# Hybrid attention layer: compressed keys and values as a fifth seven-product pair, other homes for its sums, one compression input on GpSimd

## Chip, core and metric

The kernel runs on one core of a Trainium2 chip. The metric is the device time of one execution in microseconds, median of the runs. Everything is float32 at full precision.

## What is computed

One decoder layer on 1024 tokens of width 1024: native sparse attention (NSA) and latent attention (MLA) side by side, merged by sigmoid gates, then a gated FFN with a short convolution. The change concerns the projections of the first half:

```python
h = _rmsnorm(x, g_pre_mix[i])
proj = h @ w_in[i]
q_n, kv_n, gate_n, c_q, c_kv, k_r, merge = jnp.split(proj, offsets, axis=-1)
...
def compress(k, pos, w1, b1, w2):
    kb = k[:, blk] + pos[None, None, :, None, :]
    kb = kb.transpose(0, 1, 3, 2, 4).reshape(B, n_cmp, G, CMP_BLOCK * dh)
    return jax.nn.gelu(kb @ w1 + b1) @ w2
k_cmp = compress(kc, pos_k, ck_w1, ck_b1, ck_w2)
v_cmp = compress(vc, pos_v, cv_w1, cv_b1, cv_w2)
...
gm = jax.nn.sigmoid(merge.astype(jnp.float32)).astype(x.dtype).reshape(B, T, 2, D)
merged = gm[:, :, 0] * (o_nsa @ w_br_nsa[i]) + gm[:, :, 1] * (o_mla @ w_br_mla[i])
```

kc and vc are columns 512 to 639 and 640 to 767 of `w_in`; the merge gates are 16 blocks of 128 columns from column 1720.

## The kernel before, in words

**Precision.** TensorE multiplies float32 tiles rounded to a shorter format. To keep full precision each operand is split into a rounded high part and a low rest, and each product is three matmuls: high by high, low by high, high by low (`mm3`, lines 303 to 305). The split is a pair: ScalarE writes the high part, VectorE subtracts (`split_evac`, lines 308 and 309; for whole weights lines 106 and 107, tiles whi and wlo). h, transposed, stays in SBUF as hh and hl in two halves of 512 tokens.

**Weights.** One queue in the order of use, loaded by SP into three raw buffers (wraw, 512 KB each). A whole projection of a 128-column block, `fproj`, is 8 x 3 matmuls for each half of the tokens, 48 in all. For gates that fill in between other work it is cut into eight quarters of six matmuls each, which `some(n)` hands out.

**Seven products.** Two 128-column blocks together go through class `Seven`: a pair is treated as a 2 x 2 block product that needs seven block products instead of eight, each 4 x 3 matmuls, 84 per pair. The data side needs sums T1 to T4 of h's blocks (lines 736 to 753, split into T1h, T1l and so on); the weight side needs sums S0 to S3 (line 170), which like the plain weight halves are split into a ring of four rh and rl; the outputs are put together by VectorE (line 194) in two tiles `gms`. Four pairs of gates (`gates7.pair`) are done so, then sent through a sigmoid and stored to DRAM (gm_d).

**Order around the change.** First the MLA branch: q blocks (six matmuls each) with quarters of gates between them, then k and v blocks (three matmuls each) with quarters, each split into one of six store buffers (st) and stored by SP (qn_d, qr_d, k_d, v_d). Then the last quarters, the four gate pairs, the projections of kc and vc into kcT0 and kcT1, and for keys and values in turn: `cmp_build` (loads, a transpose of pos, and kb = kcT + pos, four operations of 64 x 1008, line 858), the projection of other k columns (`k_evac`, into KA and KB), and `cmp_mm`, 16 float32 matmuls that the page counts as 32 instructions (line 865). Then the eight values blocks (V), `cmp_out` (lines 868 to 879: the second step of the compression and its splits into KAc, KBc, Vc), the q projections and the attention. GpSimd prepares constant rows of KB, KBc and of QB (lines 891 to 901 and 949 to 955).

A scheduler orders each engine's instructions; each engine then runs its own in that order and waits where an input or a buffer is not ready. Tiles get addresses from stacks on the left and the right side, so a tile can lie where an earlier one lay, and its first writer waits for the last user of that memory, stores to DRAM included.

Of the kernel before, what the change touches and what calls it, by code (L numbers as in the profile page):

```python
# [17 lines left out]
T = 1024  # L18
# [257 lines left out]
def tile_hybrid_layer(ctx: ExitStack, tc: tile.TileContext, x, p, positions, g_pre_mix, w_in,  # L276
# [85 lines left out]
    for c0 in [512, 640, 768, 1024]:  # L362
        W.add(Item(in_cols(c0), 1024))
# [404 lines left out]
    for i in range(4):  # L768
        c, g = i // 2, i % 2
        for f, n in ((q_nope(2 * g, c), 1), (q_rope(g, c), 2), (q_nope(2 * g + 1, c), 1)):  # L770
            f()
            some(n)
# [15 lines left out]

    ringA = Pool("ringA", side="left")
    tB = Pool("tB", side="left")  # L790
    for n in ("T3", "T4"):
        BA[n] = [tB([128, 4, 512], F32R, n + tag) for tag in "hl"]
    gates7 = Seven(nc, W, gate_pairs, ringA, BA, mm3, split_evac)
    t_first(2)()
    some(4)
    t_first(3)()
    some(4)
# [6 lines left out]
    for f in range(len(gate_pairs)):  # L804
        tl = [gmp([128, T], F32, "gms", bufs=2) for _ in range(2)]
        gates7.pair(f, two_banks(), bank, lambda shape, dt, name: eA(shape, dt, "t2", bufs=4), [(c[:, :512], c[:, 512:]) for c in tl],
                    lambda out_, ps: nc.scalar.activation(out_, ps, AF.Sigmoid), lambda s: None)
        nc.scalar.activation(tl[1], tl[1], AF.Sigmoid)
        nc.scalar.dma_start(gm_d[PAIRED[2 * f + 1]], tl[1])
        nc.scalar.activation(tl[0][:, 512:], tl[0][:, 512:], AF.Sigmoid)  # L810
        nc.scalar.dma_start(gm_d[PAIRED[2 * f]], tl[0])
    for pl in (tB, ringA, tA, eA):
        pl.close()
# [15 lines left out]
    kcT = [cp([128, T], F32, f"kcT{n}") for n in range(2)]  # L829
    for n in range(2):  # L830
        fproj(lambda c, cs, ps, n=n: nc.scalar.activation(kcT[n][:, cs], ps, AF.Copy))

    kbs, w1s, b1s = [], [], []

    def cmp_build(n):
        pos, w1, b1, w2 = ((nsa_pos_k, nsa_ck_w1, nsa_ck_b1, nsa_ck_w2),
                           (nsa_pos_v, nsa_cv_w1, nsa_cv_b1, nsa_cv_w2))[n]
        pl = cp([32, 2, 64], F32, f"pos{n}")
        nc.scalar.dma_start(pl[:, 0], pos[0])
        nc.scalar.dma_start(pl[:, 1], pos[0])  # L840
        w1t = cp([128, 16, 64], F32, "w1t")
        nc.scalar.dma_start(w1t, dap(w1, 0, [[64, 128], [128 * 64, 16], [1, 64]]))
        nc.scalar.dma_start(w2s[n][:, 0], w2[0])
        nc.scalar.dma_start(w2s[n][:, 1], w2[0])
        b1t = cp([64, 1], F32, f"b1t{n}")
        nc.scalar.dma_start(b1t, dap(b1, 0, [[1, 64], [1, 1]]))
        ps = bank()
        nc.tensor.transpose(ps[:, :32], pl.rearrange("p a b -> p (a b)"), ident[:32, :32])
        posT = cp([128, 32], F32, f"posT{n}")
        nc.vector.tensor_copy(posT, ps[:, :32])  # L850
        kb = cp([128, 16, 126], F32, "kb")
        for g in range(2):
            for par in range(2):
                src = kcT[n][g * 64:(g + 1) * 64, :]
                src = bass.AP(tensor=src.tensor, offset=src.offset + par,
                              ap=[list(src.ap[0]), [2, 16], [16, 63]])
                pp = posT[g * 64:(g + 1) * 64, par:32:2]
                nc.vector.tensor_tensor(kb[par * 64:(par + 1) * 64, :, g * 63:(g + 1) * 63], src,
                                        pp[:, :, None].to_broadcast([64, 16, 63]), op=OP.add)
        kbs.append(kb), w1s.append(w1t), b1s.append(b1t)  # L860
# [56 lines left out]
    for t in range(NT):  # L917
        ps = bank()
        for k in range(NK):
            mm3(ps[:, :256], tok(hh, k, t), tok(hl, k, t), w2[k // 4][0][:, k % 4], w2[k // 4][1][:, k % 4],  # L920
                k == 0, k == NK - 1)
        v = VV[t // 4][:, t % 4]
        split_evac(v[:, :, 0:64], v[:, :, 64:128], ps[:, :256].rearrange("p (a b) -> p a b", b=64))
    cmp_out()
# [998 lines left out]
```

## Time and profile before

| | |
|---|---|
| median of 3 runs | 1753.53 us (1749.5 to 1753.94) |
| profiled execution, its own time | 1752.63 us |
| its span | 1750.8 us |
| busy: TensorE, VectorE, ScalarE, GpSimd | 1694.3, 1262.1, 851.7, 304.1 us |
| mean granted clock of TensorE | 0.99 |

In the profile PE is TensorE's matmuls and PEld its weight loads, DVE is VectorE, ACT ScalarE, POOL GpSimd, SP the engine that issues most DMAs. A row of the timeline gives start and duration in us, engine, line, operation, output<-inputs, shape, count and, in brackets, how long the engine was idle before and what released it. TensorE's rows overlap: a 128x512 matmul lasts 0.39 us and the next starts after 0.23. In a table of stretches the engines come in the order PE, PEld, DVE, ACT, POOL.

### The profile page before, as it was taken

The numbers are of one execution on the slowest core, as the hardware profiler recorded it, in microseconds if no ns is written. First come the engines' busy times: TensorE is split into PE (matmuls) and PEld (weight loads), VectorE is DVE, ScalarE is ACT, GpSimd is POOL, SyncE is SP. The second block draws the span as 40 slices with busy tenths as digits, with TensorE's granted clock in tenths as the row PEclk, the third lists the DMA queues.
The fourth block names the chain that finished last, engine by engine and source line by source line (L and its number), as shares of the span: only waits on it lengthen the run. The fifth ranks groups of instructions, "written<-read, shape, count | busy, mean of one in ns | idle before, by whom it ended". The sixth has DMA issues, their size and how long they took to land.

```text
span 1750.8 us, 23413 instructions
## 1 busy us (share of the span) xinstructions
PE 1694.3 (97%) x8468; PEld 1394.1 (80%) x8468; DVE 1262.1 (72%) x1981; ACT 851.7 (49%) x1537; POOL 304.1 (17%) x446
## 2 busy tenths in 40 slices
PE   8999999999999999998999999999999999999998
PEld 6887888887777888886778877888888877887786
DVE  5667735238989888777755797888888779868543
ACT  5434423237777677666432454444444454335321
POOL 4100022014555453333211000000000000001110
PEclk9999999999999999999999999999999999999999
DMA  5266332100003237656462122222222393437111
GB/s 198 66 238 229 104 108 57 37 30 13 1 1 91 73 95 184 156 155 182 136 217 84 57 64 73 84 85 76 84 94 73 112 316 125 143 122 255 58 61 48
DMA packets 166670, 191.93 MB, mean 110 GB/s; under 512 B 13348, under 2 KB 116188, under 8 KB 166556
## 3 DMA queue, kind: packets, MB, share of 16 engines
q1 hardware_dynamic: 158732, 178.29, 33.0%
q10 hardware_dynamic: 7824, 12.16, 2.0%
q8 instruction: 67, 1.10, 0.3%
q14 instruction: 47, 0.39, 0.1%
HBM read 142.96 MB, written 47.45 MB: 109 GB/s over the span
## 4 chain that ended last, share of the span: by engine, by line
PE 78%; DVE 9%; DMA 5%; ACT 3%; issue 2%; POOL 1%; SPq 0%; DVEq 0%; POOLq 0%; ACTq 0%
PE big L303 9%; PE big L304 9%; PE big L305 9%; PE pT L303 6%; PE pT L305 6%; PE pT L304 5%; PE oT L1015 5%; PE pT L999 4%; PE one L303 3%; PE one L304 3%; PE one L305 3%; PE sc L305 2%; PE sc L303 2%; PE sc L304 2%; DVE wlo L309 2%
## 5 line engine op out<-in xcount | busy, mean ns | idle before, releaser
L345 POOL TENSOR_SCALAR stat<-stat 128x1 f32<-128x1 f32 (+1 forms) x48 | 15.0, 313 | 887.9 <-ACT yn L1404 633.6
L303 PE MATMUL big<-hh,rh 128*128 128x512 f32 x380 | 148.2, 390 | 2.5 <-ACT e L220 1.0
L304 PE MATMUL big<-hl,rh 128*128 128x512 f32 x380 | 148.0, 389 | 0.0
L305 PE MATMUL big<-hh,rl 128*128 128x512 f32 x380 | 147.5, 389 | 0.0
L309 DVE TENSOR_TENSOR pl<-pT,ph 128x512 fp32r<-128x512 f32 x228 | 139.1, 626 | 11.4 <-ACT ph L308 9.5
L308 ACT ACTIVATE ph<-pT 128x512 fp32r<-128x512 f32 x228 | 120.6, 553 | 47.7 <-PE pT L999 36.0
L983 DVE TENSOR_REDUCE mx<-sc 128x1 f32<-128x640 f32 (+7 forms) x128 | 106.6, 835 | 28.9 <-PE sc L1068 19.8
L308 ACT ACTIVATE rh<-S 128x512 fp32r<-128x512 f32 x96 | 60.3, 629 | 110.1 <-PE big L304 78.0
L1527 DVE SCALAR_TENSOR_TENSOR u<-C,wcT,u 128x1024 f32<-128x1024 f32 x88 | 110.9, 1280 | 3.7 <-ACT u L1523 3.2
L308 ACT ACTIVATE rh<-wraw 128x512 fp32r<-128x512 f32 x80 | 50.0, 630 | 107.7 <-PE big L304 47.1
L304 PE MATMUL big<-wlo,whi 128*128 128x512 f32 x242 | 95.5, 395 | 5.8 <-DVE wlo L309 5.8
L305 PE MATMUL big<-whi,wlo 128*128 128x512 f32 x242 | 94.9, 392 | 0.0
L303 PE MATMUL big<-whi 128*128 128x512 f32 x242 | 91.5, 394 | 1.7 <-ACT whi L308 1.7
L303 PEld LDWEIGHTS big<-hh,rh 128*128 128x128 f32 x380 | 71.2, 188 | 18.6 <-ACT e L220 1.5
L304 PEld LDWEIGHTS big<-hl,rh 128*128 128x128 f32 x380 | 71.3, 188 | 15.1 <-DVE hl L309 0.4
L305 PEld LDWEIGHTS big<-hh,rl 128*128 128x128 f32 x380 | 71.3, 188 | 14.7
L309 DVE TENSOR_TENSOR rl<-S,rh 128x512 fp32r<-128x512 f32 x96 | 65.7, 688 | 20.2 <-ACT rh L308 20.1
L303 PE MATMUL pT<-hh,whi 128*128 128x512 f32 x176 | 69.7, 396 | 2.3 <-DVE KBc L874 2.0
L308 ACT ACTIVATE whi<-wraw 128x1024 fp32r<-128x1024 f32 x40 | 42.1, 1058 | 59.8 <-DVE wraw L1593 25.9
L305 PE MATMUL pT<-hh,wlo 128*128 128x512 f32 x176 | 69.4, 394 | 0.0
L304 PE MATMUL pT<-hl,whi 128*128 128x512 f32 x176 | 69.2, 393 | 0.0
L309 DVE TENSOR_TENSOR rl<-wraw,rh 128x512 fp32r<-128x512 f32 x80 | 54.7, 687 | 11.4 <-ACT rh L308 11.4
(565 smaller groups left out, 5044.3 us busy)
## 6 DMA issues: line engine op xcount, KB each, us to landing
wraw<-in_w_up_dram SPq DMA_DIRECT2D x44, 512.0 KB, 4.0
wraw<-in_w_in_dram SPq DMA_DIRECT2D x24, 512.0 KB, 4.5
g<-gm_d SPq DMA_DIRECT2D x48, 256.0 KB, 3.5
wraw<-in_w_down_dram SPq DMA_DIRECT2D x47, 256.0 KB, 3.5
g_d<-u SPq DMA_DIRECT2D x22, 512.0 KB, 2.6
wraw<-g_d SPq DMA_DIRECT2D x36, 256.0 KB, 3.0
gm_d<-gms ACTq DMA_DIRECT2D x16, 512.0 KB, 2.9
xt<-in_x_dram SPq DMA_DIRECT2D x14, 512.0 KB, 3.7
```

Of the source, the lines that this page charges most:

```text
L303: nc.tensor.matmul(ps, lh, rh, start=start, stop=False, skip_group_check=more)
L304: nc.tensor.matmul(ps, lh, rl, start=False, stop=False, skip_group_check=more)
L305: nc.tensor.matmul(ps, ll, rh, start=False, stop=stop, skip_group_check=more)
L308: nc.scalar.activation(hi, ps, AF.Copy)
L309: nc.vector.tensor_sub(lo, ps, f32(hi))
L345: nc.gpsimd.tensor_scalar(st, st, EPS, None, op0=OP.add)
L983: nc.vector.tensor_reduce(u.nm[:, r:r + 1], src, axis=AX.XY, op=OP.max, negate=True)
L999: nc.tensor.transpose(pT[:m, r], cols(r), ident)
L1015: nc.tensor.matmul(oT[:, a:], v, part_, start=first and not j, stop=last and j == len(parts) - 1)
L1527: nc.vector.scalar_tensor_tensor(u[s], C[s][:, 2 - sh:2 - sh + T], wcT[:, 2 - sh, ch:ch + 1], u[s], op0=OP.mult, op1=OP.add)
```

## The change

Columns 512 and 640 leave the list of whole projections and become a fifth pair of `Seven`; its evacuation copies where the others take the sigmoid, and its two output tiles are kcT. The quarters between the q blocks become one each (12 instead of 16), those at the end six and six (12 instead of 8). T3 and T4 are taken from the stack before the ring, T4 first. The twelve loads of `cmp_build` go from ScalarE's queue to SP's, with buffers of their own for w1t and kb. The values' kb is computed on GpSimd. `cmp_out` is called at the fourth of the values blocks instead of after the eighth.

```diff
     gate_pairs = [[W.add(Item(in_cols(1720 + 128 * m), 1024, custom=True)) for m in (m_, m_ + 1)] for m_ in PAIRED[::2]]
-    for c0 in [512, 640, 768, 1024]:
+    gate_pairs.append([W.add(Item(in_cols(c0), 1024, custom=True)) for c0 in (512, 640)])
+    for c0 in [768, 1024]:
         W.add(Item(in_cols(c0), 1024))
...
-        for f, n in ((q_nope(2 * g, c), 1), (q_rope(g, c), 2), (q_nope(2 * g + 1, c), 1)):
+        for f in (q_nope(2 * g, c), q_rope(g, c), q_nope(2 * g + 1, c)):
             f()
-            some(n)
+            some(1)
...
+    tB = Pool("tB", side="left")
+    for n in ("T4", "T3"):
+        BA[n] = [tB([128, 4, 512], F32R, n + tag) for tag in "hl"]
     ringA = Pool("ringA", side="left")
-    tB = Pool("tB", side="left")
-    for n in ("T3", "T4"):
-        BA[n] = [tB([128, 4, 512], F32R, n + tag) for tag in "hl"]
     gates7 = Seven(nc, W, gate_pairs, ringA, BA, mm3, split_evac)
     t_first(2)()
-    some(4)
+    some(6)
     t_first(3)()
-    some(4)
+    some(6)
...
+        way = AF.Copy if f == 4 else AF.Sigmoid
         gates7.pair(f, two_banks(), bank, lambda shape, dt, name: eA(shape, dt, "t2", bufs=4), [(c[:, :512], c[:, 512:]) for c in tl],
-                    lambda out_, ps: nc.scalar.activation(out_, ps, AF.Sigmoid), lambda s: None)
+                    lambda out_, ps: nc.scalar.activation(out_, ps, way), lambda s: None)
+        if f == 4:
+            kcT = tl
+            break
...
-    kcT = [cp([128, T], F32, f"kcT{n}") for n in range(2)]
-    for n in range(2):
-        fproj(lambda c, cs, ps, n=n: nc.scalar.activation(kcT[n][:, cs], ps, AF.Copy))
...
-        w1t = cp([128, 16, 64], F32, "w1t")
-        nc.scalar.dma_start(w1t, dap(w1, 0, [[64, 128], [128 * 64, 16], [1, 64]]))
-        nc.scalar.dma_start(w2s[n][:, 0], w2[0])
-        nc.scalar.dma_start(w2s[n][:, 1], w2[0])
+        w1t = cp([128, 16, 64], F32, f"w1t{n}")
+        nc.sync.dma_start(w1t, dap(w1, 0, [[64, 128], [128 * 64, 16], [1, 64]]))
+        nc.sync.dma_start(w2s[n][:, 0], w2[0])
+        nc.sync.dma_start(w2s[n][:, 1], w2[0])
...
-        kb = cp([128, 16, 126], F32, "kb")
+        kb = cp([128, 16, 126], F32, f"kb{n}")
...
-                nc.vector.tensor_tensor(kb[par * 64:(par + 1) * 64, :, g * 63:(g + 1) * 63], src,
+                (nc.gpsimd if n else nc.vector).tensor_tensor(kb[par * 64:(par + 1) * 64, :, g * 63:(g + 1) * 63], src,
                                         pp[:, :, None].to_broadcast([64, 16, 63]), op=OP.add)
...
+        if t == 3:
+            cmp_out()
         v = VV[t // 4][:, t % 4]
         split_evac(v[:, :, 0:64], v[:, :, 64:128], ps[:, :256].rearrange("p (a b) -> p a b", b=64))
-    cmp_out()
```

The lines after the change stand one or two further down than before. At three places the order of an engine's rows carries the argument.

ScalarE from the split of the last v block (the st row of shape 128x8x64) to the ring's first splits, before. DMAHW and a number is the completion of a transfer on one of the DMA rings, the other names are engines; gms is a finished half of a gate.

```order
L308 ACTIVATE st<-pT 128x8x64 [waits DMAHW5_49,DVE_49,PE_49]
L629 ACTIVATE gms<-sc 128x512 [waits PE_49]
L631 DMA gm_d<-gms 128x1024 [waits Activation_49]
L308 ACTIVATE T3h<-e 128x512 [waits DMAHW3_49,DMAHW4_49,DMAHW2_49,DVE_49]
L308 ACTIVATE T4h<-t_1471 128x512
L308 ACTIVATE rh<-wraw 128x512 [waits DMAHW0_49]
L308 ACTIVATE rh<-wraw 128x512 [waits DMAHW7_49]
L308 ACTIVATE rh<-S_1623 128x512 [waits DVE_49]
```

And in the changed kernel:

```order
L308 ACTIVATE st<-pT 128x8x64 [waits DMAHW3_49,PE_49]
L630 ACTIVATE gms<-sc 128x512 [waits PE_49]
L632 DMA gm_d<-gms 128x1024 [waits DMAHW4_49,Activation_49]
L630 ACTIVATE gms<-sc 128x512 [waits DMAHW5_49,PE_49]
L308 ACTIVATE T3h<-e 128x512 [waits DMAHW7_49,DMAHW0_49,DVE_49]
L308 ACTIVATE T4h<-t_1445 128x512
L308 ACTIVATE rh<-wraw 128x512 x2
L308 ACTIVATE rh<-S_1623 128x512 [waits DVE_49]
L308 ACTIVATE rh<-S_1617 128x512
L630 ACTIVATE gms<-sc 128x512 [waits PE_49]
```

Before, two halves of a gate and its store stand ahead of T3h; now the second half comes after the ring's splits, and T3h waits on other transfers.

VectorE at the values' kb (kb_2493, before); KB10 and KB11 are split from the second k columns, and wlo belongs to the values' weights.

```order
L858 TENSOR_TENSOR kb_2493<-kcT1_2227,posT1_2491 64x16x63 x3
L887 TENSOR_TENSOR KB01_2209<-pT_2431,KA01_2205 64x512
L858 TENSOR_TENSOR kb_2493<-kcT1_2227,posT1_2491 64x16x63
L887 TENSOR_TENSOR KB10_2210<-pT_2504,KA10_2206 64x512
L887 TENSOR_TENSOR KB11_2211<-pT_2504,KA11_2207 64x512
L107 TENSOR_TENSOR wlo_2598<-wraw_2297,whi_2597 128x1024
L887 TENSOR_TENSOR KB10_2210<-pT_2535,KA10_2206 64x512
L887 TENSOR_TENSOR KB11_2211<-pT_2535,KA11_2207 64x512
```

GpSimd in the changed kernel at the same place, from the constant rows of KBc to the first row of the attention's preparation.

```order
L902 TENSOR_SCALAR KBc0_2354<-jrow_2366 1x64
L902 TENSOR_SCALAR KBc1_2355<-jrow_2366 1x64
L897 MEMSET KB00_2348 1x1024
L898 TENSOR_SCALAR KB00_2348<-jrow_2366 1x1024
L897 MEMSET KB01_2349 1x1024
L898 TENSOR_SCALAR KB01_2349<-jrow_2366 1x1024
L897 MEMSET KB10_2350 1x1024
L898 TENSOR_SCALAR KB10_2350<-jrow_2366 1x1024
L897 MEMSET KB11_2351 1x1024
L898 TENSOR_SCALAR KB11_2351<-jrow_2366 1x1024
L859 TENSOR_TENSOR kb1_2514<-gms_2216,posT1_2512 64x16x63 x4
L969 TENSOR_SCALAR QB10_3125<-QA1_2616 64x512
```

kb1 has left VectorE's rows and stands on GpSimd behind all the constant rows of KB.

VectorE around `cmp_out` (KBc and Vc), before; V1 is the second half of the values, wlo the weights of the first q columns.

```order
L309 TENSOR_TENSOR V1_2596<-pT_2738,V1_2596 128x4x64
L309 TENSOR_TENSOR V1_2596<-pT_2765,V1_2596 128x4x64
L107 TENSOR_TENSOR wlo_2839<-wraw_2398,whi_2838 128x1024
L309 TENSOR_TENSOR V1_2596<-pT_2792,V1_2596 128x4x64
L107 TENSOR_TENSOR wlo_2845<-wraw_2502,whi_2844 128x1024
L874 TENSOR_TENSOR KBc0_2214<-pT_2819,KAc0_2212 64x63
L309 TENSOR_TENSOR Vc0_2198<-pT_2825,Vc0_2198 63x64
L309 TENSOR_TENSOR Vc1_2199<-pT_2831,Vc1_2199 63x64
L874 TENSOR_TENSOR KBc1_2215<-pT_2819,KAc1_2213 64x63
```

And in the changed kernel:

```order
L309 TENSOR_TENSOR V0_2340<-pT_2705,V0_2340 128x4x64
L875 TENSOR_TENSOR KBc0_2354<-pT_2730,KAc0_2352 64x63
L309 TENSOR_TENSOR Vc0_2338<-pT_2736,Vc0_2338 63x64
L875 TENSOR_TENSOR KBc1_2355<-pT_2730,KAc1_2353 64x63
L309 TENSOR_TENSOR Vc0_2338<-pT_2736,Vc0_2338 63x64
L309 TENSOR_TENSOR Vc1_2339<-pT_2742,Vc1_2339 63x64 x2
L309 TENSOR_TENSOR V1_2617<-pT_2750,V1_2617 128x4x64
L309 TENSOR_TENSOR V1_2617<-pT_2777,V1_2617 128x4x64
L309 TENSOR_TENSOR V1_2617<-pT_2804,V1_2617 128x4x64
L107 TENSOR_TENSOR wlo_2860<-wraw_2419,whi_2859 128x1024
L309 TENSOR_TENSOR V1_2617<-pT_2831,V1_2617 128x4x64
```

The two wlo that stood ahead of the first KBc row now stand after the Vc rows, with three V rows between.

## Rows read from the trace of the kernel before

**Rows 1.** The page's busy times, and the chain that ended last by engine.

```profile
PE 1694.3 (97%) x8468; PEld 1394.1 (80%) x8468; DVE 1262.1 (72%) x1981; ACT 851.7 (49%) x1537; POOL 304.1 (17%) x446
...
PE 78%; DVE 9%; DMA 5%; ACT 3%; issue 2%; POOL 1%; SPq 0%; DVEq 0%; POOLq 0%; ACTq 0%
```

**Rows 2.** Stretches: length, busy us of each engine (instructions), granted clock, DMA share, GB/s.

```profile
162.00:172.00 10.00, 6.09 (x14) 4.31 (x15) 7.42 (x13) 5.13 (x10) 0.00 (x0) 0.66 0.51 158
172.00:232.00 60.00, 60.00 (x266) 49.65 (x265) 41.94 (x65) 26.12 (x42) 0.00 (x0) 1.00 0.35 106
```

**Rows 3.** The chain that ended last, 157 to 167 us: start, us, what.

```profile
157.43 6.38 DMA v_d<-st
...
163.91 0.64 ACT T3h L308
...
164.58 0.59 DVE T3l L309
...
166.47 0.61 DVE rl L309
```

**Rows 4.** TensorE's timeline, 155 to 172 us: start, us, what, [idle before <-releaser].

```profile
155.59 0.39 PE L305 MATMUL pT<-wvh,ctl 128*128 128x512 f32 x1
...
161.61 0.39 PE L305 MATMUL sc<-hh,wlo 128*128 128x512 f32 x1
165.64 0.80 PE L303 MATMUL sc<-hh,rh 128*128 128x512 f32 x1 [3.64 <-ACT rh L308]
...
171.99 0.40 PE L304 MATMUL pT<-hl,rh 128*128 128x512 f32 x1
```

**Rows 5.** The timelines of TensorE and of VectorE around `cmp_out`.

```profile
320.25 0.28 PE L305 MATMUL pT<-whi,hl 128*128 128x256 f32 x1
...
321.88 0.33 PE L877 MATMUL pT<-w2t,gl 64*63 64x64 f32 x2 [0.69 <-DVE V L309]
324.19 0.47 PE L303 MATMUL pT<-hh,whi 128*128 128x512 f32 x1 [1.98 <-DVE KBc L874]
...
329.07 0.40 PE L305 MATMUL pT<-hh,wlo 128*128 128x512 f32 x1
...
320.27 1.23 DVE L107 TENSOR_TENSOR wlo<-wraw,whi 128x1024 fp32r<-128x1024 f32 x1 [1.74 <-ACT whi L106]
...
321.92 1.23 DVE L107 TENSOR_TENSOR wlo<-wraw,whi 128x1024 fp32r<-128x1024 f32 x1
```

**Rows 6.** Stretches of the q section and of the last stores, columns as above.

```profile
115.00:120.00 5.00, 5.00 (x24) 4.14 (x23) 4.83 (x8) 0.91 (x2) 0.00 (x0) 1.00 0.24 91
156.00:162.00 6.00, 5.75 (x24) 4.43 (x24) 2.92 (x5) 0.68 (x2) 0.00 (x0) 1.00 1.02 365
```

**Rows 7.** The chain that ended last at the first compression.

```profile
278.48 3.60 PE pT L865 x32
```

**Rows 8.** Groups of GpSimd and VectorE, shapes apart, and line 955 (ns min/median/max).

```profile
L965 POOL TENSOR_TENSOR QB<-QB,inc 1x512 fp32r<-1x512 f32 x12 | 12.4, 1032 | 12.1 <-PE sc L1035 8.6 <-PE sc L1037 3.1
L1332 POOL TENSOR_TENSOR g<-g,g 128x512 f32<-128x512 f32 x8 | 11.1, 1393 | 23.7 <-DVE g L1330 8.3 <-DVE pl L309 7.9 <-DMA g<-gm_d 7.6
...
L313 POOL TENSOR_TENSOR oml<-osum,omh 64x512 fp32r<-64x512 f32 x8 | 10.7, 1333 | 12.2 <-ACT omh L312 12.2
...
L313 POOL TENSOR_TENSOR wol<-wlo,woh 128x1024 fp32r<-128x1024 f32 x1 | 3.4, 3397 | 0.0
...
L309 DVE TENSOR_TENSOR rl<-S,rh 128x512 fp32r<-128x512 f32 x96 | 65.7, 688 | 20.2 <-ACT rh L308 20.1
...
L858 DVE TENSOR_TENSOR kb<-kcT,posT 64x1008 f32<-64x1008 f32 x8 | 15.1, 1890 | 0.2
...
L955 POOL TENSOR_SCALAR QB<-PC x16: 288/290/1867, 254.6 to 273.5; 1x128 fp32r<-1x128 f32 x16
```

**Rows 9.** GpSimd's timeline, the last of four fills of KB.

```profile
263.90 0.95 POOL L896 MEMSET KB<- 1x1024 f32 x1
264.91 1.04 POOL L897 TENSOR_SCALAR KB<-jrow 1x1024 fp32r<-1x1024 f32 x1
```

More of the change, by code (lines that the diff above doesn't have):

```diff
@@ L811, in tile_hybrid_layer @@
         nc.scalar.dma_start(gm_d[PAIRED[2 * f]], tl[0])
-    for pl in (tB, ringA, tA, eA):
+    for pl in (ringA, tB, tA, eA):
         pl.close()
@@ L838, in cmp_build @@
         pl = cp([32, 2, 64], F32, f"pos{n}")
-        nc.scalar.dma_start(pl[:, 0], pos[0])
-        nc.scalar.dma_start(pl[:, 1], pos[0])
-        w1t = cp([128, 16, 64], F32, "w1t")
-        nc.scalar.dma_start(w1t, dap(w1, 0, [[64, 128], [128 * 64, 16], [1, 64]]))
-        nc.scalar.dma_start(w2s[n][:, 0], w2[0])
-        nc.scalar.dma_start(w2s[n][:, 1], w2[0])
+        nc.sync.dma_start(pl[:, 0], pos[0])
+        nc.sync.dma_start(pl[:, 1], pos[0])
+        w1t = cp([128, 16, 64], F32, f"w1t{n}")
+        nc.sync.dma_start(w1t, dap(w1, 0, [[64, 128], [128 * 64, 16], [1, 64]]))
+        nc.sync.dma_start(w2s[n][:, 0], w2[0])
+        nc.sync.dma_start(w2s[n][:, 1], w2[0])
         b1t = cp([64, 1], F32, f"b1t{n}")
-        nc.scalar.dma_start(b1t, dap(b1, 0, [[1, 64], [1, 1]]))
+        nc.sync.dma_start(b1t, dap(b1, 0, [[1, 64], [1, 1]]))
         ps = bank()
```

## The prediction

> **What bounds the kernel now.** The page's busy table and its chain of work that ended last come first [rows 1]: TensorE is busy 1694.3 of 1750.8 us, and the chain spends most of its time on it. A change pays here only by taking matmuls away or by closing one of TensorE's few holes. The second view is the table of stretches [rows 2]. From 172 to 232 us (four seven-product pairs) TensorE is busy all the time, 266 matmuls in 60 us, so one costs 0.2256 us. Two stretches around it have holes: 162 to 172 us holds 14 matmuls at a granted clock of 0.66, and a second one follows at 321 us. The change touches both.
>
> The first hole is read from the chain and from TensorE's timeline [rows 3, 4]. The last V store of the MLA branch is issued at 157.43 and takes 6.38 us. Only then does ScalarE split T3 (163.91), since T3h lies where the last store buffers lay; the ring's rh splits stand behind T3h, and TensorE starts the first product at 165.64, after 3.64 us idle and at half clock (0.43 us between matmuls, 1.2 instead of 2.4 GHz) until 171.99. From the start of the last matmul before (161.61) to that of the fourteenth after (171.99) are 10.38 us; fourteen pitches are 3.16. **The hole costs 7.2 us.**
>
> The second is `cmp_out` [rows 5]. VectorE does two whole-tile wlo splits (320.27 and 321.92, 1.23 us each) ahead of the small KBc and Vc subtractions; TensorE is idle 0.69 and 1.98 us and then runs at half clock to 329.07. From 320.25 to 329.07 are 8.82 us, in which stand one 128x256 matmul (0.12), the six tiny ones (about 0.5) and fourteen of 0.2256 (3.16): **5.0 us lost.**
>
> **The change, term by term.**
>
> *Fifth pair.* Columns 512 and 640 were two whole projections of 48 matmuls each; as a pair they are 7 x 4 x 3 = 84. Twelve matmuls fewer at 0.2256: **-2.7 us**. VectorE's sums and ScalarE's ring splits of a fifth pair cost nothing as long as that pair runs like the four before it, where TensorE never waited [rows 2].
>
> *Homes and covers.* T4 and T3 now lie below the ring. T3h waits for the stores that were fourth to sixth from the end, T3l on VectorE for the last one, and the ring's rh no longer waits behind a gate's second half: the row order shows gms, T3h, T4h and four rh ahead of it. Four quarters (24 matmuls) move from the q section to the tail, so that after the last V matmul 46 matmuls stand ahead of the first product, 10.4 us, instead of 24. Call the end of that V matmul V: 155.98 in the trace [rows 4], its store issued at V+1.45 and landed at V+7.9. T3l, T4l, S3 and the first rl are queued on VectorE in this order, 0.6 us apart and 0.69 long [rows 3]: the first rl is done at about V+10.5. The first product's third matmul, the one that needs it, comes at V+10.85. It fits, by a third of a microsecond. A ring load on SP now waits for three of the stores and holds up the loads behind it; it serves the sums of the second pair, which VectorE reaches some nine operations after the first rl, and by standing behind the stores it no longer shares the queues with them. I leave 0.5 us of the 7.2: **-6.7**, bounds -7.2 and -2 (landing 2 to 3 us later, with part of the half clock). The q section loses 5.4 us of cover; in its fullest stretch VectorE was 97% busy and TensorE waited for nothing [rows 6], so I price that at nothing; if that stretch sets the pace it is a microsecond or two.
>
> *`cmp_out` inside the values, at t == 3.* No wlo stands ahead of its subtractions any more; the two wlo come behind three more V rows. Between the tiny matmuls and the subtractions a short wait stays. I leave 1 us of the 5.0: **-4.0**, bounds -5 and -2.
>
> *Compression loads on SP.* ScalarE loses twelve DMA issues, which stood around its first kcT copy, and the four copies. TensorE did not wait for either, so this is worth nothing. On SP the group stands ahead of the next q weights and waits with w2t until the fifth pair is over; those weights are wanted only after the eight values, more than 40 us on. Nothing again.
>
> *kb of the values on GpSimd.* This is the term against the change. Call E the end of the fifth pair's last product. TensorE then has a tiny transpose, k columns (48 matmuls, 10.9 us), the first compression (32 matmuls, 3.6 us, [rows 7]), a transpose with a wait of 0.35, 48 more matmuls: the second compression comes due at E+26.2, and it needs kb1. GpSimd cannot begin it early, for the row order puts it last: the QB rows (their buffers and PC's lie over T4, which the fifth pair reads to E-5.4, and wait for VectorE's memsets up to E+0.2) end near E+1.9, jrow 0.98, four memsets of 0.95 (E+6.7), two KBc rows, each of which I expect to be held by one of VectorE's kb0 operations, as the QB rows were (1867 ns at most, 290 in the median, [rows 8]) (E+9.7), then four fills of 0.95 and 1.04 with 0.1 between the rows, and something for VectorE's splits beside them (E+18.3). In the kernel before, all these fills ran beside the two projections that are now gone [rows 9]. Four kb operations follow. The trace has none on GpSimd. VectorE takes 1890 ns for one; GpSimd's two-input rows are 1333 ns for 64x512 and 1393 for 128x512 [rows 8], so by elements 2.6 us (1333 x 1008/512). Bounds: 2.1 (its 1x512 row of 1032 gives 2.0, and a little for 64 partitions) and, by VectorE's time and the two engines' ratio at 128x512 (1393/688 = 2.02), 3.8. VectorE's kb is slower per element than its plain rows, since its source is strided; whether GpSimd also slows down is open. I take 2.6, the row with the same partitions. With one hold of about 0.6 us by the wlo that VectorE does in that stretch, kb1 is ready at E+18.3+10.4+0.6 = E+29.3: TensorE idle 3.1 us. What an idle of this length costs beside itself is read from both holes: 7.2 lost at 3.64 idle, 5.0 at 0.69+1.98, so 2.3 to 3.6 more; I take 2.4. **+5.5**, bounds 0 and +11.2 (second rival).
>
> The Trainium skill ("GPSIMD Engine Reference", sections 3.1 and 4.1) says that two-input elementwise work is about twice as slow on GpSimd as on VectorE and should stay on the latter; the ratio of the rows, 2.02, agrees, and by it a kb operation would take 3.8 us (second rival below). "SBUF — State Buffer" says that the two engines lock each other out of a shared port pair for whole instructions; the QB rows of 1867 ns beside kb agree.
>
> **Sum.** -2.7 - 6.7 - 4.0 + 5.5 = -7.9 against the profiled execution's own 1752.63: 1744.7. The median of the runs is 0.9 above that execution, so the forecast is **1746** (1745.6). A difference of 0.3%, 5.3 us, is about what a measurement of this kernel can tell from none.
>
> **Rivals.**
> 1. *kb1 is not late.* At 2.1 us and with the KBc rows not held (3 us saved), kb1 is ready at E+24.3, before TensorE comes. For it: the fills' own time is known only from a stretch in which VectorE disturbed them. -13.4, so 1740. Chance 0.20.
> 2. *kb1 is late by far.* At 3.8 us an operation it is ready at E+34.1; idle 7.9 and 3.3 of half clock take 11.2: -2.2, so 1751, no change that can be told. For it: VectorE's own slowness on this access. Against: GpSimd's per-element time is already twice VectorE's, which leaves room for a stride to hide in. Chance 0.20.
> 3. *The last store still holds the first product.* If it lands at V+10.5 rather than V+7.9 (from 156 to 162 us the DMA engines are full, 1.02, [rows 6]), the first rl is 2.3 us late: with some half clock 3.5 of the 6.7 are given back: -4.4, so 1749. Against: the load that shared the queues now waits. Chance 0.08.
> 4. *Slower.* kb1 at 5.7 us or more an operation. Then kb1 is ready at E+41.7, idle 15.5 and 3.3: -13.4+18.8 = +5.4; at 6 us +6.6, so 1760. For it only the GpSimd row of 3397 ns for 128x1024, times the stride's factor on VectorE (1890 against 688 x 1008/512 = 1354, 1.4) 4.7: that gives +1.4 and still no loss. Chance 0.07.
>
> **How the numbers follow.** The forecast has 0.45 (1743 to 1747.5 by its small bounds). Faster: the forecast and rival 1, 0.65; same: rivals 2 and 3, 0.28; slower: rival 4, 0.07. The range runs from rival 1's 1739 to rival 2 with a microsecond above, 1752.5.
>
> **What would show it.** The stretch from the last V matmul to the fifth product without a hole, granted clock 1.0, T3l on VectorE right after the v_d landing; TensorE's instructions fewer by twelve ahead of the values; at `cmp_out` an idle of at most 1 us. The decisive row is the first matmul of the second compression: its idle, released by GpSimd's kb, near 3 us, and four GpSimd rows of about 2.6 us. The prediction is wrong if that idle is absent or above 7 us, or if TensorE waits for T3l or rl with the last store behind it.

## The result and the profile after

| | before | changed |
|---|---|---|
| median of 6 runs each | 1752.22 us (1749.5 to 1753.94) | 1738.45 us (1736.27 to 1739.95) |
| profiled execution, its own time; its span | 1752.63; 1750.8 us | 1737.69; 1735.7 us |
| mean granted clock of TensorE | 0.990 | 0.994 |

The ratio is 0.9923 [0.991, 0.9936]: faster by 13.8 us, where 1746 (1739 to 1752.5) was forecast. The sign was right, the size was not: the measured time lies just below the range. In later runs beside the experiments the kernel before had medians of 1748.3 to 1750.1, the changed one 1738.94 (ratio 0.9935 [0.9918, 0.9951]), so about 11 us is the better figure of what the change is worth, and the 7.9 of the sum was some 3 us short of it. Where both come from is taken apart below.

The page's busy times and the chain by engine, of the changed kernel, answer to [rows 1]:

```profile
PE 1685.6 (97%) x8456; PEld 1386.6 (80%) x8456; DVE 1262.2 (73%) x1991; ACT 855.1 (49%) x1540; POOL 311.3 (18%) x450
...
PE 78%; DVE 9%; DMA 5%; ACT 3%; issue 2%; POOL 2%; SPq 0%; DVEq 0%; POOLq 0%; ACTq 0%
```

TensorE has twelve instructions fewer; GpSimd has four more, the kb rows. TensorE's waits from 95 to 345 us, in which every edit lies (for each releaser: us in total, times, longest):

```profile
PE sc L303 <- ACT gms L630: 0.7, 1, 0.7
PE sc L303 <- ACT gms L809: 0.7, 1, 0.7
PE pT L303 <- DVE KBc L875: 0.5, 1, 0.5
PE pT L866 <- POOL kb L859: 0.4, 1, 0.4
PE pT L303 <- DVE posT L851: 0.3, 1, 0.3
PE pT L878 <- DVE V L309: 0.3, 1, 0.3
```

The 3.64 for rh and the 1.98 for KBc [rows 4, 5] are gone, and no wait is longer than 0.7. Two waits of 0.69 are new in size: one for the evacuation of the last quarters (line 630), one in the fifth pair (line 809). The forecast's decisive row is the fourth: GpSimd's kb holds TensorE for 0.4 us, not for 3.1.

The first hole, in the timelines of ScalarE, VectorE and TensorE after the last V matmul (its end, V, is 151.97):

```profile
157.48 0.62 ACT L308 ACTIVATE T3h<-e 128x512 fp32r<-128x512 f32 x1
...
158.37 0.69 DVE L309 TENSOR_TENSOR T3l<-e,T3h 128x512 fp32r<-128x512 f32 x1 [3.24 <-DMA gm_d<-gms]
...
160.18 0.69 DVE L309 TENSOR_TENSOR rl<-wraw,rh 128x512 fp32r<-128x512 f32 x1
...
162.98 0.39 PE L305 MATMUL sc<-hh,wlo 128*128 128x512 f32 x1
163.21 0.39 PE L303 MATMUL sc<-hh,rh 128*128 128x512 f32 x1
```

T3l follows 0.3 us after T3h's end, and the first product starts one pitch (0.23) after the last quarter's matmul, with no idle and no half clock. Its first rl is done at 160.87, and the third matmul that needs it comes at 163.66: 2.8 us to spare, where the forecast had a third of one. Two things that it did not have made the difference. T3l starts at V+6.4, not at V+7.9: the profile names a gate's store as what released it, and if it waits for the last V store too, as the forecast has it, that one (issued at 153.35) took at most 5.0 us, against 6.38 [rows 3]. And TensorE comes 0.8 later, most of it the wait of 0.69 for the last quarters.

The values' kb on GpSimd, in its timeline:

```profile
257.52 2.59 POOL L957 TENSOR_SCALAR QB<-PC 1x128 fp32r<-1x128 f32 x8
260.18 0.98 POOL L892 IOTA jrow<- 1x1024 f32 x1
...
264.83 2.61 POOL L902 TENSOR_SCALAR KBc<-jrow 1x64 fp32r<-1x64 f32 x2
...
276.55 9.92 POOL L859 TENSOR_TENSOR kb<-gms,posT 64x1008 f32<-64x1008 f32 x4
```

And the two compressions in TensorE's:

```profile
270.76 3.67 PE L866 MATMUL pT<-kb,w1t 128*64 128x126 f32 x32
...
286.53 3.67 PE L866 MATMUL pT<-kb,w1t 128*64 128x126 f32 x32 [0.44 <-POOL kb L859]
```

E, the end of the fifth pair, is 259.55 here. The QB rows end at E+0.6 (forecast 1.9), from jrow to kb1's start go 16.4 us as forecast, kb1 takes 9.9 instead of 10.4 and is held by nothing, since VectorE's two wlo stand ahead of it (272.35) and behind it (286.99): ready at E+26.9, where 29.3 was forecast. TensorE comes at E+26.5. The second compression's 32 matmuls take 3.67 us like the first's: after 0.44 us the clock is still whole.

`cmp_out` in TensorE's timeline answers to [rows 5]:

```profile
301.82 0.48 PE L871 MATMUL pT<-gl,w2t 64*128 64x126 f32 x2
302.24 0.32 PE L878 MATMUL pT<-w2t,gl 64*63 64x64 f32 x2
302.83 0.32 PE L878 MATMUL pT<-w2t,gl 64*63 64x64 f32 x2 [0.27 <-DVE V L309]
303.69 0.36 PE L303 MATMUL pT<-whi,hh 128*128 128x256 f32 x1 [0.54 <-DVE KBc L875]
```

The two waits are 0.81 us instead of 2.67, and the clock stays whole behind them. The two wlo now stand behind the V rows, and the first one just holds the first q projection, in TensorE's and VectorE's timelines:

```profile
316.02 0.40 PE L304 MATMUL pT<-hl,whi 128*128 128x512 f32 x1
316.48 0.50 PE L305 MATMUL pT<-hh,wlo 128*128 128x512 f32 x1
...
315.20 1.23 DVE L107 TENSOR_TENSOR wlo<-wraw,whi 128x1024 fp32r<-128x1024 f32 x1 [1.75 <-ACT whi L106]
```

The matmul that needs wlo starts 0.46 us after the one before it instead of 0.23, and 0.05 after the split's end.

To place the gain, the same matmul, counted from the program's end, is looked up in each trace; its start minus its start in the profile of before is what that kernel has gained (-) or lost up to there, in us. The differences between neighbouring columns belong to one stretch. The first column is the place of the last V block in the kernel before, the second the fifth pair's start, the last the program's last matmul. Since the places are counted from the end, a kernel with twelve matmuls fewer shows their 2.7 us in the first column already, though they are left out in the fifth pair. (The whole first column moves with how the program's first 30 us went; the changed kernel's own profile began 0.97 late.)

| kernel | last V block | fifth pair | before the 2nd compression | behind it | q projections | end |
|---|---|---|---|---|---|---|
| changed | -1.75 | -8.61 | -7.63 | -7.11 | -10.23 | -15.37 |
| changed, again | -2.70 | -9.57 | -8.59 | -8.13 | -11.25 | -13.61 |
| before, again | +0.28 | -0.39 | -0.35 | -0.35 | -0.38 | -1.97 |
| kb on VectorE | -2.55 | -9.42 | -8.44 | -8.43 | -11.55 | -15.76 |
| 3 on GpSimd, 1 on VectorE | -2.66 | -9.53 | -8.56 | -8.55 | -11.68 | -14.33 |
| one more kb | -2.40 | -9.26 | -8.29 | -3.67 | -6.80 | -13.25 |
| three more kb | -2.40 | -9.27 | -8.27 | +2.00 | -1.13 | -4.48 |
| cmp_out last | -2.58 | -9.45 | -8.47 | -7.95 | -8.17 | -6.52 |
| old homes | -2.60 | -9.47 | -0.42 | -0.26 | -3.37 | -6.79 |
| old quarters | -2.44 | -3.75 | -2.78 | -2.28 | -5.39 | -8.70 |
| cmp_out alone | +0.04 | -1.26 | -1.26 | -1.26 | -4.40 | -9.84 |
| pair alone | -2.17 | -1.92 | +7.33 | +7.33 | +8.21 | +1.09 |
| loads on ScalarE | -2.53 | -9.40 | -8.39 | -7.92 | -11.07 | -14.47 |

The pair itself, from its first matmul to the position transpose, against the two projections of the kernel before:

```profile
245.26 0.39 PE L303 MATMUL pT<-hh,whi 128*128 128x512 f32 x1
...
267.11 0.24 PE L848 MATMUL pT<-ident,pos 32*128 32x32 f32 x1
```

```profile
239.37 0.39 PE L303 MATMUL pT<-T2h,rh 128*128 128x512 f32 x1
...
259.48 0.24 PE L849 MATMUL pT<-ident,pos 32*128 32x32 f32 x1
```

20.11 us in place of 21.85: 1.7 less, which is twelve matmuls (2.7) less and 1.0 more.

In the changed kernel: -2.7 for the twelve matmuls (by the program; the column shows it less the late start), -6.9 at the first product, +1.0 within the fifth pair (a wait of 0.69 of its last product for ScalarE's copy of a finished half, gms at line 809, and what goes with it), +0.5 at the second compression, -3.1 at `cmp_out`: **-11.2 ahead of the q projections.** Behind them both kernels run the same instructions, and still the difference moves by -5.1 in this profile; in the other twelve it moved by -7.1 to +1.7, and mostly downwards: the profile of before was a late one there.

### The profile page after: what moved, and what is told of

The parts are those of the page before. It is cut to its first block, busy times and chain, and to the rows that moved or that the text cites. A ratio compares the mean times of both kernels' runs of the same rounds, so it can differ in the third digit from the quotient of the medians.

```text
span 1735.7 us, 23425 instructions
## 1 busy us (share of the span) xinstructions
PE 1685.6 (97%) x8456; PEld 1386.6 (80%) x8456; DVE 1262.2 (73%) x1991; ACT 855.1 (49%) x1540; POOL 311.3 (18%) x450
## 4 chain that ended last, share of the span: by engine, by line
PE 78%; DVE 9%; DMA 5%; ACT 3%; issue 2%; POOL 2%; SPq 0%; DVEq 0%; POOLq 0%; ACTq 0%
PE big L303 10%; PE big L304 10%; PE big L305 10%; PE oT L1017 5%; PE pT L303 5%; PE pT L305 5%; PE pT L304 5%; PE pT L1001 4%; PE one L303 3%; PE one L304 3%; PE one L305 3%; PE sc L303 2%; PE sc L305 2%; PE sc L304 2%; DVE wlo L309 1%
## 5 line engine op out<-in xcount | busy, mean ns | idle before, releaser
L304 PEld LDWEIGHTS big<-wlo,whi 128*128 128x128 f32 x242 | 45.4, 188 | 19.0 <-DVE wlo L309 9.9
L309 DVE TENSOR_TENSOR wlo<-wraw,whi 128x1024 fp32r<-128x1024 f32 x40 | 48.7, 1224 | 14.0 <-ACT whi L308 13.4
L1017 PE MATMUL oT<-ph,V 128*128 128x512 f32 x132 | 56.7, 429 | 1.1 <-DVE osum L1154 0.7
```

Source lines behind the costliest of these rows:

```text
L304: nc.tensor.matmul(ps, lh, rl, start=False, stop=False, skip_group_check=more)
L309: nc.vector.tensor_sub(lo, ps, f32(hi))
L1017: nc.tensor.matmul(oT[:, a:], v, part_, start=first and not j, stop=last and j == len(parts) - 1)
```

## The experiments

All edits are to the changed kernel, unless it says to the kernel before. The ratio is to the kernel before, run on the same chip.

**1. The values' kb back on VectorE.**

```diff
-                (nc.gpsimd if n else nc.vector).tensor_tensor(kb[par * 64:(par + 1) * 64, :, g * 63:(g + 1) * 63], src,
+                nc.vector.tensor_tensor(kb[par * 64:(par + 1) * 64, :, g * 63:(g + 1) * 63], src,
```

> The changed kernel with the values' kb back on VectorE; all else as changed. Theory A (the change's gain is the sum of its other terms, and GpSimd's kb comes almost on time and costs 0.4 us of TensorE's time): TensorE's 0.44 us wait before the second compression goes, the total stays within 1 us of the changed kernel's 1738.5. Rival B (taking four operations of 1.9 us off VectorE is itself a source of the gain, since KB's subtractions and the values' weights stood behind them): those rows come late again, TensorE waits at the first values block or at the second compression, and the total is 3 us or more above, 1741.5 or higher.

1738.0 us, ratio 0.9936 [0.9918, 0.9955]. The wait of 0.44 is gone, and the stretch with the second compression is 0.5 us shorter. VectorE does these four rows from 274.06 on, in a hole of its own, and they delay nobody. The theory held, the rival did not: the move costs half a microsecond and brings nothing.

**2 and 3. kb1 made late:** in run 2 one of the four GpSimd operations is done twice, in run 3 three of them. The repeated operation writes the same values.

```diff
+                for _ in range(2 - min(1, g + par) if n else 1):
-                (nc.gpsimd if n else nc.vector).tensor_tensor(kb[par * 64:(par + 1) * 64, :, g * 63:(g + 1) * 63], src,
+                    (nc.gpsimd if n else nc.vector).tensor_tensor(kb[par * 64:(par + 1) * 64, :, g * 63:(g + 1) * 63], src,
...
```

In run 3 the first added line is:

```diff
+                for _ in range(1 + max(g, par) if n else 1):
...
```

> The changed kernel with the first of the four values' kb operations computed twice on GpSimd, so that kb1 comes about 2.45 us later. This makes the idle of about 3 us that the prediction expected. Theory A (the step that failed is when GpSimd gets there; the price of an idle of 3 us, itself and 2.4 us of half clock behind it, was right): idle 2.9 us, granted clock below 1.0 behind it, total up by 4 to 5 us, 1743. Rival B (the half clock does not follow here, since the 32 narrow matmuls come first): idle 2.9, clock 1.0, total up by 2.5 us, 1741.

> The changed kernel with three of the four values' kb operations computed twice on GpSimd: kb1 comes about 7.3 us later. Theory A (idle and half clock as the prediction priced them for its second rival): idle 7.8 us and some 3.3 us of half clock, total up by 10.6 us less the 0.4 that is there already, 1748 to 1749. Rival B (no half clock): up by 7.3 us, 1746.

With one more: 1741.78 us, ratio 0.9951 [0.9935, 0.9967]. With three: 1749.69, ratio 0.9994 [0.9981, 1.0006]. The second compression on TensorE's timeline with one more, and the stretch around it (length, busy us of each engine, granted clock, DMA):

```profile
288.32 5.33 PE L867 MATMUL pT<-kb,w1t 128*64 128x126 f32 x32 [2.89 <-POOL kb L860]
```

```profile
286.00:296.00 10.00, 7.68 (x52) 7.51 (x53) 4.40 (x3) 3.03 (x6) 2.26 (x1) 0.83 0.19 52
```

The same stretch in the changed kernel, at whole clock:

```profile
286.00:296.00 10.00, 9.56 (x82) 9.30 (x82) 3.03 (x4) 4.07 (x7) 0.47 (x1) 1.00 0.19 54
```

And with three more, with GpSimd's seven kb operations (ns min/median/max) and the wlo that VectorE does beside them:

```profile
294.07 5.24 PE L867 MATMUL pT<-kb,w1t 128*64 128x126 f32 x32 [8.62 <-POOL kb L860]
...
L860 POOL TENSOR_TENSOR kb<-gms,posT x7: 2352/2437/3222, 275.9 to 291.7; 64x1008 f32<-64x1008 f32 x7
...
286.35 3.02 DVE L107 TENSOR_TENSOR wlo<-wraw,whi 128x1024 fp32r<-128x1024 f32 x1 [2.42 <-ACT whi L106]
```

With one more the idle grows by just what is added (2.45), with three by 8.2 instead of 7.3: one of its operations, beside the wlo, takes 3222 ns, and the wlo takes 3.02 us, against 1.23 in the changed kernel. A hold of this kind, of 0.6 us, the forecast had put into the changed kernel. At 2.89 us of idle, close to the forecast's 3.1, the 32 matmuls take 5.33 us instead of 3.67. From the column before the second compression to the one behind it the two kernels lose 4.1 and 9.8 us more than the changed one: 2.45 and 8.2 of idle and 1.6 for the clock. So a late kb1 costs what the forecast said it would in kind, idle and half clock, though the clock's part was put too high (2.4, and 3.3 in the second rival; measured 1.6, and no more after 8.6 us than after 2.9); that kb1 would be late by so much was wrong. By its times run 2 is 3.3 us above the changed kernel's 1738.5, between the theory's 4 to 5 and the rival's 2.5; the clock of 0.83 in the trace decides for the theory.

**4. `cmp_out` back behind the values.**

```diff
-        if t == 3:
-            cmp_out()
...
+    cmp_out()
```

> The changed kernel with cmp_out after the eight values blocks again. Theory A (the two whole-tile splits ahead of the small subtractions made the hole, so it returns): TensorE idle 0.7 and 2.0 us and at half clock behind it, total up by 3 to 4 us, 1742. Rival B (the hole had to do with what the kernel before did around it, and with GpSimd's kb out of the way the splits come earlier): total within 1 us of the changed kernel's 1738.5.

1743.59 us, ratio 0.9966 [0.9953, 0.9979]. TensorE's waits of before return, and the granted clock with them, in the table of waits and the stretch around it:

```profile
PE pT L303 <- DVE KBc L875: 2.0, 1, 2.0
PE pT L878 <- DVE V L309: 0.7, 1, 0.7
```

```profile
312.00:321.00 9.00, 6.33 (x26) 4.91 (x26) 3.94 (x9) 2.63 (x9) 0.00 (x0) 0.81 0.43 117
```

Up to the q projections it costs 2.9 us, as expected. By the times it is 5.1, above the expected 3 to 4; the rest lies behind the q projections, where this profile gains nothing.

**5. `cmp_out` alone, in the kernel before.**

```diff
+        if t == 3:
+            cmp_out()
...
-    cmp_out()
```

> The kernel before with cmp_out called at the fourth values block and nothing else. Theory A (it is worth what undoing it in the changed kernel cost there, 2.9 us): TensorE's waits of 0.7 and 2.0 us at cmp_out shrink to below 1 us, no half clock, total 2.5 to 3.5 us below the kernel before. Rival B (in the kernel before VectorE is late at the fourth block, since it also does the values' kb): below 1 us gained.

1747.3 us, ratio 0.9989 [0.9979, 0.9999]. The waits are the 0.3 and 0.5 of the changed kernel, and the stretch gains 3.1 us. The edit is worth the same with or without the others. Its times say less than its trace: the interval allows a gain of 0.2 to 3.7 us.

**6. Old quarters, new homes:** one, two and one between the q blocks, four and four at the end.

```diff
-        for f in (q_nope(2 * g, c), q_rope(g, c), q_nope(2 * g + 1, c)):
+        for f, n in ((q_nope(2 * g, c), 1), (q_rope(g, c), 2), (q_nope(2 * g + 1, c), 1)):
             f()
-            some(1)
+            some(n)
...
-    some(6)
+    some(4)
...
-    some(6)
+    some(4)
```

> The changed kernel with the quarters handed out as before (16 in the q section, 8 at the end); the new homes stay. Theory A (the cover closes the hole): 24 matmuls after the last V matmul, 5.4 us, while T3l on VectorE still waits for the last store until V+8 and the first rl is ready near V+10.5; TensorE idle 4 to 5 us at the third matmul of the first product, half clock behind it, total up by 6 to 7 us, 1745. Rival B (the homes close it): idle below 1 us, total within 1.5 us of the changed kernel's 1738.5.

1744.98 us, ratio 0.997 [0.9956, 0.9984]. TensorE's timeline at the first product:

```profile
165.24 0.50 PE L303 MATMUL sc<-hh,rh 128*128 128x512 f32 x1 [2.96 <-ACT rh L308]
...
166.75 0.50 PE L305 MATMUL sc<-hh,rl 128*128 128x512 f32 x1 [0.78 <-DVE rl L309]
```

The homes alone bring 1.3 of the 6.9 us, and the same stretch, untouched, differs by as much between other profiles (0.7 in the second of before, 1.3 with `cmp_out` alone). The wait for rh stays at 2.96, and rl is late behind it: the cover is needed, as the theory had it. But it is no store that makes rh late, as ScalarE's timeline shows:

```profile
163.51 0.63 ACT L308 ACTIVATE T3h<-e 128x512 fp32r<-128x512 f32 x1 [0.60 <-ACT gms L630]
```

T3h stands behind the last quarters' evacuation (162.31 to 162.91) and the issue of their store. The new homes may have taken the stores out of the way; with the old quarters the order of ScalarE's rows then holds the first product about as long.

**7. Old homes, new quarters:** the ring taken before T3 and T4, T3 first.

```diff
+    ringA = Pool("ringA", side="left")
     tB = Pool("tB", side="left")
-    for n in ("T4", "T3"):
+    for n in ("T3", "T4"):
...
-    ringA = Pool("ringA", side="left")
...
-    for pl in (ringA, tB, tA, eA):
+    for pl in (tB, ringA, tA, eA):
```

> The changed kernel with T3 and T4 over the ring again, as before; the 46 matmuls of cover stay. Theory A (the longer cover closes the hole at the first product, the homes add little): ScalarE's T3h waits for the last store, landed near V+8, and the first rh is ready before TensorE comes at V+10.4, the first rl about as late as it is needed; TensorE idle below 1 us there, total within 1.5 us of the changed kernel's, 1738 to 1740. Rival B (the homes close the hole): idle above 2.5 us with half clock behind it, total up by 4 us or more, 1742 and above.

1748.56 us, ratio 0.9989 [0.9978, 1.0001]. At the first product there is no hole. T3h still waits for a store, as ScalarE's timeline shows, but the new quarters alone cover it, whatever the homes:

```profile
157.46 0.63 ACT L308 ACTIVATE T3h<-e 128x512 fp32r<-128x512 f32 x1 [0.73 <-DMA v_d<-st]
```

The theory was right there. But 9 us are lost behind the fifth pair, which no expectation had. TensorE's timeline from the position transpose to the second one:

```profile
254.93 0.24 PE L849 MATMUL pT<-ident,pos 32*128 32x32 f32 x1
255.10 0.50 PE L303 MATMUL pT<-hh,whi 128*128 128x512 f32 x1
...
260.00 0.39 PE L303 MATMUL pT<-hh,whi 128*128 128x512 f32 x1
260.22 0.39 PE L303 MATMUL sc<-hh,rh 128*128 128x512 f32 x1
...
262.71 0.39 PE L305 MATMUL sc<-hh,rl 128*128 128x512 f32 x1
...
274.96 5.34 PE L866 MATMUL pT<-kb,w1t 128*64 128x126 f32 x32 [5.96 <-DVE kb L859]
281.47 0.22 PE L849 MATMUL pT<-ident,pos 32*128 32x32 f32 x1 [1.17 <-issue]
```

And VectorE's:

```profile
263.20 0.69 DVE L194 TENSOR_TENSOR gms<-sc,t 128x512 f32<-128x512 f32 x1 [7.80 <-PE sc L305]
263.94 1.57 DVE L954 MEMSET QB<- 64x512 f32 x3
...
266.94 7.96 DVE L859 TENSOR_TENSOR kb<-gms,posT 64x1008 f32<-64x1008 f32 x4
```

The scheduler has put 22 of the k column's matmuls ahead of the last twelve of the fifth pair (the sc rows from 260.22). Those twelve finish kcT, so kb0 starts at 266.94 instead of 261.62, while the work that would have covered it is spent. In the changed kernel all k columns stand behind E, and 48 matmuls cover kb0. So once the new quarters are there, what the homes change is another thing than the forecast thought: not the wait for the stores, but which matmuls the scheduler places behind the pair.

**8. The fifth pair alone, in the kernel before:** the pair, its copy and the `break`, with the loads, kb, quarters, homes and `cmp_out` of before.

```diff
+    gate_pairs.append([W.add(Item(in_cols(c0), 1024, custom=True)) for c0 in (512, 640)])
-    for c0 in [512, 640, 768, 1024]:
+    for c0 in [768, 1024]:
...
+                    lambda out_, ps: nc.scalar.activation(out_, ps, AF.Copy if f == 4 else AF.Sigmoid), lambda s: None)
+        if f == 4:
+            kcT = tl
+            break
...
-    kcT = [cp([128, T], F32, f"kcT{n}") for n in range(2)]
-    for n in range(2):
-        fproj(lambda c, cs, ps, n=n: nc.scalar.activation(kcT[n][:, cs], ps, AF.Copy))
```

> The kernel before with columns 512 and 640 as a fifth pair and nothing else: homes, quarters, loads on ScalarE's queue, kb on VectorE and cmp_out stay. Theory A (twelve matmuls fewer, 2.7 us, less a new wait of about 0.7 us for a gate tile): total 1.5 to 3 us below the kernel before. Rival B (without the two projections the constant rows on GpSimd, kb on VectorE and the loads on ScalarE's queue lose their cover): a new wait of TensorE of 2 us or more at the compression, total the same as before or above.

1754.31 us, ratio 1.0024 [1.0014, 1.0033]: slower, as the rival had it. Of its three reasons one shows, VectorE's kb; TensorE waits for no constant row and no load. The first compression in TensorE's timeline:

```profile
282.72 5.10 PE L866 MATMUL pT<-kb,w1t 128*64 128x126 f32 x32 [6.16 <-DVE kb L859]
289.24 0.21 PE L849 MATMUL pT<-ident,pos 32*128 32x32 f32 x1 [1.42 <-issue]
```

It is the loss of run 7 again, 9.25 us, with the same order (23 k matmuls ahead of the last twelve products). Twelve matmuls fewer are worth 2.7 only where the order behind them holds.

**9. The twelve loads of `cmp_build` back on ScalarE's queue.**

```diff
-        nc.sync.dma_start(pl[:, 0], pos[0])
+        nc.scalar.dma_start(pl[:, 0], pos[0])
...
```

> The changed kernel with the twelve loads of cmp_build issued by ScalarE again (w1t and kb keep a buffer for each half). Theory A (moving them to SP was worth nothing, as predicted): TensorE's waits ahead of the q projections as in the changed kernel within 0.5 us, total 1738 to 1740. Rival B (on ScalarE's queue they now stand behind the fifth pair's evacuation and ahead of the KA copies, so that pos or KA comes late): a new wait of TensorE of 1 us or more at the transposes of pos or at the compression, total 1741 or more.

1738.65 us, ratio 0.9945 [0.9928, 0.9961], and up to the q projections the row of the table is that of the changed kernel's second profile within 0.2 us: worth nothing, as forecast.

**10. Three kb rows on GpSimd, the last on VectorE,** the version that the runs pointed to.

```diff
-                (nc.gpsimd if n else nc.vector).tensor_tensor(kb[par * 64:(par + 1) * 64, :, g * 63:(g + 1) * 63], src,
+                (nc.gpsimd if n and g + par < 2 else nc.vector).tensor_tensor(kb[par * 64:(par + 1) * 64, :, g * 63:(g + 1) * 63], src,
```

> The changed kernel with three of the values' four kb operations on GpSimd and the fourth on VectorE, which has nothing to do then. Theory A: kb1 is ready 2.4 us earlier, TensorE's 0.44 us wait before the second compression goes, nothing else moves: ahead of the q projections 0.5 us below the changed kernel, the total the same within what the times can tell. Rival B (the two engines hold each other up, and KB's subtractions on VectorE come late): a wait of TensorE of 1 us or more at the compression or the first values block.

1737.29 us, ratio 0.9928 [0.9909, 0.9948]. The wait is gone and the trace shows 0.4 us for it; by the times it is the changed kernel (1738.94 on the same chip).

**11 and 12. Both kernels once more, unchanged.**

> The kernel before once more, unchanged, for a second profile. Up to the q projections the profiles so far differ by the edits alone; behind them the same instructions took up to 6.5 us less and 1.7 us more than in the first profile of before. Theory A (chance within one program: the same short waits are or aren't followed by half clock): the stretch from the attention to the end differs from that of the first profile of before by 2 us or more, although nothing was changed. Rival B (it hangs on what the change does ahead of it): it agrees within 1 us.

> The changed kernel once more, unchanged, for a second profile and more times beside the others'. Theory A: the part ahead of the q projections agrees with the first profile within 0.2 us but for the first 30 us of the program, the part behind them differs by 1 us or more. Rival B: both agree within 0.5 us. The total 11 to 13 us below the kernel before.

Before: 1750.66 in one execution; changed: 1738.94, ratio 0.9935 [0.9918, 0.9951]. Ahead of the q projections the two profiles of the changed kernel agree from column to column within 0.1 us, behind them they differ by 2.8, as the theory had it. The second profile of before differs from the first by 1.6 behind the q projections, between the 2 us or more of the theory and the 1 us of the rival. It shows what chance does there, with not one instruction changed. The stretch of 444 to 456 us, first in the profile that the forecast was made from:

```profile
444.00:456.00 12.00, 10.88 (x73) 8.87 (x72) 10.68 (x24) 8.68 (x19) 6.86 (x8) 1.00 0.00 0
```

and in the second:

```profile
444.00:456.00 12.00, 10.88 (x62) 8.87 (x62) 9.22 (x23) 7.81 (x17) 6.17 (x8) 0.86 0.00 0
```

TensorE waits for hl for 1.1 us in this stretch in both. In one the clock stays whole behind it, in the other it falls to 0.86, and 11 matmuls fewer get done; the second profile loses 1.6 us there, and elsewhere it is the first that loses. Over all 19 runs on one chip the kernel before took 1744.8 to 1754.8 us.

## Why the prediction was wrong in size and right in sign

- **The failed step is the +5.5 for kb on GpSimd,** in it the moment at which kb1 is ready; the trace shows +0.5 (0.44 of idle and no loss of clock). No single estimate was far off. From E the QB rows ended 1.3 us earlier, kb1 took 0.5 less (2437 ns a row, [rows 8] gave 2.6 us), the wlo that was to hold it for 0.6 came after it, and TensorE came 0.3 later: 2.7 us together, nearly all of the 3.1 idle, and the clock's 2.4 went with them. All four fell on the same side, and the price does not shrink in step: runs 1 to 3 show 1.6 us for the clock at 2.89 us of idle and none at 0.44.
- **The first rival** (kb1 not late, -13.4, 1740) came nearest by its number, not by its mechanism. It had 2.1 us a row and the KBc rows not held, so kb1 ready at E+24.3. The rows took 2.44, the two KBc rows were held (2.61 us together), kb1 was ready at E+26.9, and TensorE did wait. Its reason was weak too: the fills of [rows 9] ran while VectorE was idle (6.26 us, until 267.39), and from jrow to kb1 the time came out as forecast. The range began at 1739, a microsecond below that rival's own 1740, and the measured 1738.45 lies under both.
- **-2.7 for twelve matmuls:** right by the count (96 matmuls became 84). But the sentence that the fifth pair runs like the four before it was not quite so: +1.0 by its end, where its last product waits 0.69 for ScalarE's copy of a finished half; the sum had put that at nothing. And the pair is only worth something because the k columns follow it; with the old homes 9 us are lost at the same place (runs 7 and 8). The forecast had no such term, since the order of the changed kernel already had the columns behind E.
- **-6.7 at the first product:** -6.9 measured; the working was right in its cover and wrong in what the homes do. Run 6 has the homes without the cover: 1.3 of 6.9 at most. Run 7 has the cover without the homes: all of it. The homes do their work behind the fifth pair. That the size fits so well is in part luck: the first rl had 2.8 us to spare and not a third of one, and the 0.5 that was left for it went into a wait of 0.69 that the forecast did not have.
- **-4.0 at `cmp_out`:** -3.1; mis-sized by 0.9. The forecast left 1 us of the 5.0; by its own way of counting 1.9 are left. Start to start in TensorE's rows they are 0.81 of waits, 0.6 because the six tiny matmuls take 1.06 us by themselves where it had put about 0.5, 0.4 at the first q matmuls, where the wlo now comes late, and the rest beside the tiny ones. For the wlo ahead of the q projections it had no term. Runs 4 and 5 give 2.9 and 3.1 for the same edit.
- **0 for the loads, 0 for the thinner q section:** right (run 9; from 95 us on no wait in the q section in the table of waits).
- **The rest of the miss** is the starting point. Measured from piece to piece the sum is -11.2 in place of -7.9. Taken from the later medians of the kernel before (1748.3 to 1750.1) it gives 1737.1 to 1738.9, and the changed kernel's two medians are 1738.45 and 1738.94. The forecast took its sum from 1753.5, the median of three runs that came out 3 to 5 us above the later ones; whether chance or the chip did that is not on record. Between the first two profiles the same instructions behind the q projections took 5.1 us less, in the others up to 7 us less or 1.7 more than in the profile that the forecast was made from. That such differences are chance is shown for the kernel before by its own second profile and its spread; why the clock falls behind a wait in one execution and not in another stays open.

The rule that was weighed ahead of the result, twice VectorE's time for two-input work on GpSimd (the Trainium skill, "GPSIMD Engine Reference", section 4.1), gave an estimate of 3.8 us for a kb row; the trace has 2437 ns against VectorE's 1890 [rows 8], 1.29 times, so here the measurement decides against it.

Open is also which estimate of the scheduler lets the k columns pass the pair's last products under the old homes. Its order was read and its cost measured; no run changed that order by itself.

## What to carry to other kernels

An arrival that is worked out from ten rows needs an error of its own: here four small terms came out on the same side, and a wait of 3 us shrank to 0.4. Where lateness costs something beside itself (here nothing at 0.4 us, 1.6 at 2.9), the chances should cover both cases. A rival that comes nearest by its number is worth checking by its mechanism as well. Ask of each part of a change alone what the other engines' order becomes without the rest: a pair that saves twelve matmuls was slower by itself, and the buffers' places mattered by the order that they led to, not by the stores that they waited for. And judge an edit of 3 us by its own stretch in the trace, for runs of one kernel differ by more.

## What the runs showed of the hardware that was not expected

- GpSimd's strided, broadcast add on 64 partitions took 2437 ns (2431 to 2445 over four), 1.29 times VectorE's 1890; on plain 128x512 rows the two are at 1393 and 688 [rows 8], 2.02 times. By elements VectorE's plain row gives 1354 ns for this operation and GpSimd's 64x512 row (1333) gives 2624, so VectorE is 1.4 times slower than that here and GpSimd is not slower.
- The clock's cost behind an idle did not grow with it: 32 narrow matmuls took 3.67 us after 0.44 us, 5.33 after 2.89, 5.34 after 5.96, 5.10 after 6.16 and 5.24 after 8.62.
- GpSimd and VectorE slow each other down where they meet: in run 3 one of GpSimd's kb rows took 3222 ns instead of 2437, and the wlo split on VectorE beside it 3.02 us instead of 1.23.
- The same wait of 1.1 us in the same program was followed by a granted clock of 1.00 in one execution and 0.86 in another.
